# Scores of the dilated groups 4 and 16: query parts stacked on 128 rows, keys doubled, scores emitted further behind their projections

## The chip, the core and the metric

The kernel runs on one core of a Trainium2 chip. A core has a matrix engine (TensorE, PE in the profile; its weight loads are listed apart as PEld), a vector engine (VectorE, DVE), a scalar engine (ScalarE, ACT), a general engine (GpSimd, POOL), a queue that mostly issues DMAs (SyncE, SP), and 16 DMA engines. The engines run beside each other. Each takes its own instructions in the order of the program and waits on semaphores for the others. Matrix products land in 8 banks of PSUM, everything else lies in SBUF, 128 partitions wide. The metric is the device time of one execution in microseconds (us).

## What is computed

The reference is an encoder of two layers over 512 positions of width 1024. Each layer projects its normed input, runs a multi-head latent attention (8 heads, "m" below) and a dilated window attention (three groups of 8 heads, "d" below), gates both, and projects back. The change is in the scores of two of the three dilated groups:

```
DIL_PAIRS = ((128, 1), (512, 4), (2048, 16))      # (window, dilation)

for g, (window, dil) in enumerate(DIL_PAIRS):
    q = partial_rope(qkv[:, :, g, 0], cos, sin)
    k = partial_rope(qkv[:, :, g, 1], cos, sin)
    v = qkv[:, :, g, 2]
    o, lse = banded_attention(to_strided(q, dil), to_strided(k, dil), to_strided(v, dil), window // (2 * dil))
...
s = jnp.einsum('nbqhd,nbkhd->nbhqk', qp, kw) * (Dh ** -0.5)       # Dh = 64
s = jnp.where(valid, s, -inf);  e = exp(s - max(s));  o = (e / sum(e)) v
```

A head is 64 wide, and everything is float32.

## The kernel before

**Precision.** A float32 value is kept as two parts of the faster matrix type: hi, its rounding, and lo, the rest. `split` makes them with one ACT copy (L222) and one DVE subtraction (L223). A product is then hi·hi + hi·lo + lo·hi, which `triple` issues as three matmuls (L242 to L244).

**The units of dilated attention.** `unit(u)` maps 12 units of a layer to a group g and a pair of heads p. Units 0, 1, 6, 7 are the near group (dilation 1); units 2, 3, 8, 9 (dilation 4) and 4, 5, 10, 11 (dilation 16) are the far ones, 8 in each layer. For each unit `dil_qk` projects the query and the key of the two heads (24 matmuls of 512 columns each), rotates them in `rope` (DVE L634, L635, L638, POOL L636), and splits them: the query into a tile `q` (three buffers, shared with the latent attention), the key into the one tile `kst`. In both, head a lies on partitions 64a to 64a+63, and the second index says hi or lo.

**The scores of a far unit.** `far_scores` runs twice for each unit (part 0 and 1). A part has two blocks j of 128 positions. For each block and head there is one matmul of 64 rows and 256 columns (L752: q hi against k hi and k lo) and one of 64 rows and 128 columns (L755: q lo against k hi, added to the first half). That makes 8 matmuls in a part, and 32 parts in the kernel. The two heads of a block have a bank each. DVE adds the mask (L758) and the two halves and takes the row's extreme (L761), ACT takes the exponential (L765).

**What follows.** `far_out` transposes the probabilities on PE (L457), splits them to `pt` and multiplies them with the values (L793). The latent heads do the same with L457 and L558. For dilation 16, `shares` combines the three groups' denominators, and POOL scales the probabilities (L773). `mla_out` gates a pair of latent heads (L441) and splits the result into `hl` tiles, which the output projection reads.

**What sets the order.** `Weave.run` writes the program. It walks a hand-made list of projections (`forward_order`, the main line), and behind each step emits side work that has come due: a side task may start once its needs were emitted at least a lag ago, on a clock that counts estimated PE time. The scores wait `LD` = 8.25 behind the emission of their projections (`LD0` for unit 0, `LM` for latent heads). Where the main line is blocked, side tasks are forced without regard to the lag: the key projection of unit u waits until the scores of unit u-1 are emitted, since there is only one `kst`. Weight tiles are fetched three ahead by SP, split by ACT (L199, L201), and for most of them POOL issues a second, adding DMA that makes the lo part (L202).

Of the kernel before, what the change touches and what calls it, by code (L numbers as in the profile page):

```python
# [8 lines left out]
FR = mybir.dt.float32r  # L9
I32 = mybir.dt.int32  # L10
AF = mybir.ActivationFunctionType
ALU = mybir.AluOpType
AX = mybir.AxisListType

S = 512
# [7 lines left out]
AHEAD, RATE, LAG, CAP = 3, 451.1, 2.5, 34.9  # L23
STEP, LD0, WARM, LG2, LY = 2, 10.0, 8, 16.5, 5.0
LV = 3.0
LG, LP, LD, LM, LC, LN, LX, LF = 6.0, 0.25, 8.25, 2.0, 14.25, 5.75, 5.0, 0.25
SHUF = [i + 8 if i < 8 else i - 8 if i < 16 else i for i in range(32)]

# [4 lines left out]
def unit(u):  # L33

    return u % 6 // 2, 2 * (u // 6) + u % 2
# [26 lines left out]
def F(a):  # L62
    return a.bitcast(F32)
# [74 lines left out]
def hybrid_encoder(ctx, tc, xT, wst, gains, fgain, tables, keytab, masks, out):  # L138
    nc = tc.nc
    PSUM = bass.MemoryType.PSUM  # L140
    const = ctx.enter_context(tc.tile_pool(name="const", bufs=1))
# [6 lines left out]
    def t(shape, dtype, tag, bufs):  # L148
        uid[0] += 1
        return sb.tile(shape, dtype, name=f"{tag}_{uid[0]}", tag=tag, bufs=bufs)  # L150
# [16 lines left out]
    def bank():  # L167
        uid[0] += 1
        return ps.tile([128, S], F32, name=f"bank_{uid[0]}", tag="bank", bufs=8)
# [7 lines left out]
    msk = const.tile([128, 644], F32, name="msk")  # L177
    cms = const.tile([128, 2, S], F32, name="cms")
    kcs = const.tile([128, 8, 32], F32, name="kcs")
    kst = const.tile([128, 2, S], FR, name="kst")  # L180
    kml = [const.tile([128, 2, S], FR, name=f"kml{i}") for i in range(2)]
    x1d = dram.tile([D, S], F32, name="x1d")
    shd = [[dram.tile([24, 128], F32, name=f"shd{l}{p}") for p in range(4)] for l in range(DEPTH)]
# [37 lines left out]
    def split(dst_hi, dst_lo, src):  # L221
        nc.scalar.copy(dst_hi, src)  # L222
        nc.vector.tensor_tensor(dst_lo, src, F(dst_hi), op=ALU.subtract)  # L223
# [119 lines left out]
    def half_chunks(L, key):  # L343

        a = bank()
        for i in range(2):
            w = weight(L.l, *key, i)
            for j in range(0, 4, STEP):
                cost = quads(a, w, L.h[4 * i + j:4 * i + j + STEP], 4 * i + j, 8)
                if i == 0 or j + STEP < 4:  # L350
                    yield cost, 0.0
        return a
# [295 lines left out]
    def dil_qk(L, u, qk):  # L648
        g, p = unit(u)
        a = yield from half_chunks(L, ("dqk", u, qk))  # L650
        if qk == 0:
            f = rope(L, a, "nat" if g else "queries")
            q = t([128, 2, S], FR, "q", 3)
            split(q[:, 0], q[:, 1], f)
            L.q["d", u] = q
        else:
            f = rope(L, a, "nat" if g else "keys")
            split(kst[:, 0], kst[:, 1], f)
        yield 0.65 * STEP, 0.0

    def near_scores(L, u, part):

        g, p = unit(u)
        q = L.q["d", u]
        if part == 0:
            L.st0[p] = t([128, 4, 4], F32, "st0", 2)
        st = L.st0[p]
        banks = [bank() for _ in range(2)]  # L670
        for j in range(2):
            i = 2 * part + j
            for x, (lq, lk) in enumerate(((0, 0), (0, 1), (1, 0))):
                for a in range(2):
                    r = slice(64 * a, 64 * a + 64)
                    so, k = banks[a][:, 256 * j:256 * j + 256], kst[r, lk]
                    if i:
                        k = k[:, 128 * (i - 1):128 * (i + 1)]
                    else:
                        so, k = so.rearrange("p (c x) -> p c x", c=2), k.rearrange("p (c x) -> p c x", c=4)[:, 0:4:3]  # L680
                    nc.tensor.matmul(so, q[r, lq, 128 * i:128 * i + 128], k, start=x == 0, stop=x == 2)  # L681
        for j in range(2):
            i = 2 * part + j
            m = msk[:, 0:256] if i else msk[:, 256:512]
            pt = t([128, S], F32, "p", 8)
            for a in range(2):
                pa = pt[:, 256 * a:256 * a + 256]
                nc.vector.tensor_tensor_reduce(pa, banks[a][:, 256 * j:256 * j + 256], m, -0.125, 3e38,
                                               ALU.add, ALU.min, st[:, i, a:a + 1])
            for a in range(2):  # L690
                pa = pt[:, 256 * a:256 * a + 256]
                nc.scalar.activation(pa, pa, AF.Exp, bias=st[:, i, a:a + 1], scale=-1.0,
                                     accum_out=st[:, i, 2 + a:3 + a])
            L.p["d", u, i] = pt
        if part:
            by_residue(L, p)
        yield 0.9, 1.0
# [37 lines left out]
    def far_scores(L, u, part):  # L735

        g, p = unit(u)
        q = L.q["d", u]  # L740
        st = L.st[p][:, :, g]
        m = msk[:, 512:640].rearrange("p (x y) -> p x y", y=4) if g == 1 else msk[:, 640:644].unsqueeze(1).to_broadcast([128, 32, 4])
        pt = t([128, S], F32, "p", 8)
        p4 = pt.rearrange("p (j a x) -> p j a x", j=2, a=2)
        banks = [bank() for _ in range(2)]
        by4 = lambda x: x.rearrange("p j (x y) -> p j x y", y=4)
        for j in range(2):
            b = 2 * part + j
            c = slice(128 * b, 128 * b + 128)
            for a in range(2):  # L750
                so = banks[a][:, 256 * j:256 * j + 256].rearrange("p (l x) -> p l x", l=2)
                nc.tensor.matmul(so, q[64 * a:64 * a + 64, 0, c], kst[64 * a:64 * a + 64, :, c], start=True, stop=False)  # L752
            for a in range(2):
                so = banks[a][:, 256 * j:256 * j + 128]
                nc.tensor.matmul(so, q[64 * a:64 * a + 64, 1, c], kst[64 * a:64 * a + 64, 0, c], start=False, stop=True)  # L755
        for a in range(2):
            s = banks[a].rearrange("p (j l x) -> p j l x", j=2, l=2)
            nc.vector.tensor_tensor(by4(p4[:, :, a]), by4(s[:, :, 0]), m.unsqueeze(1).to_broadcast([128, 2, 32, 4]), op=ALU.add)  # L758
            for j in range(2):
                b = 2 * part + j  # L760
                nc.vector.tensor_tensor_reduce(p4[:, j, a], s[:, j, 1], p4[:, j, a], -0.125, 3e38, ALU.add, ALU.min,  # L761
                                               st[:, b, a:a + 1])
            for j in range(2):
                b = 2 * part + j
                nc.scalar.activation(p4[:, j, a], p4[:, j, a], AF.Exp, scale=-1.0, bias=st[:, b, a:a + 1],  # L765
                                     accum_out=st[:, b, 2 + a:3 + a])
        L.p["d", u, part] = pt
        if g == 2 and part:
            shares(L, p)
            for b in range(4):  # L770
                for a in range(2):
                    pt = L.p["d", u, b // 2][:, 256 * (b % 2) + 128 * a:256 * (b % 2) + 128 * a + 128]
                    nc.gpsimd.tensor_scalar(pt, pt, L.share[p][:, b, 2, a:a + 1], 0.0, op0=ALU.mult, op1=ALU.add)  # L773
        yield 0.44, 0.5
# [161 lines left out]
    main, nline, sline, tline, cline = ([] for _ in range(5))  # L936
    for L in layers:
        l = L.l
        L.wo, L.x, L.acc, L.o = {}, [], {}, {}
        k = lambda *a: (l,) + a  # L940
        now = lambda *labels: [(x, 0.0) for x in labels]
        later = lambda *labels: [(x, LAG) for x in labels]
        task = lambda line, label, needs, f, *a: line.append((label, needs, lambda f=f, L=L, a=a: f(L, *a)))
# [3 lines left out]
        for o in ORDER:  # L947
            kind, a = o[0], o[1:]
# [8 lines left out]
            elif kind == "nv":  # L957
                task(main, k("nva", *a), now(k("norm")), near_values, a[0])
                task(nline, k(*o), [(k("nva", *a), LV)], turn_values, a[0])
            elif kind == "mv":  # L960
# [12 lines left out]
        for hd in range(8):  # L973
            p = hd // 2
# [3 lines left out]
        for u in range(12):  # L978
            g, p = unit(u)
            i = at["dqk", u, 1]  # L980
            att.append((i, ("d", u), [k("dqk", u, 0), k("dqk", u, 1), k("v", g, p // 2) if g else k("nv", p)],
                        far_scores if g else near_scores, far_out if g else near_out))
        for p in range(4):
            of = {unit(u): u for u in range(12)}
            i = at["dqk", of[2, p], 1]
            needs = later(k("s", "d", of[2, p]), *[k("o", "d", of[g, p]) for g in range(2)])
# [3 lines left out]
        before = [[], []]  # L990
        for _, (what, n), needs, scores, f in sorted(att, key=lambda x: x[0]):
            if scores:
                task(sline, k("s0", what, n), [(x, LM if what == "m" else LD0 if n == 0 else LD) for x in needs], scores, n, 0)
                task(sline, k("s", what, n), now(*before[0]), scores, n, 1)
                task(tline, k("o", what, n), [(k("s", what, n), LG2 if what == "d" and unit(n)[0] == 2 else LG)], f, n)
                before = [before[1], [("t", l, what, n)]]
            else:
                task(cline, k(what, n), needs, f, n)
# [145 lines left out]
```

## Time and profile before

| | |
|---|---|
| time, median of 3 runs | 933.5 us (932.68 to 936.16) |
| the profiled execution's own time | 936.2 us |
| its span, from first to last instruction | 934.4 us |
| mean granted PE clock in it | 0.995 |
| PE matmuls in it | 5172 |
| L752 and L755 among them | 128 and 128 |

A row of the timeline gives the start in us from the span's start, the duration in us, the engine, the line, the operation and its tiles, how many equal ones are merged, and in square brackets how long the engine stood idle before it and what ended that. A row of the groups gives the shapes (for a matmul: contraction rows * output rows, then rows x columns of the moving operand), the count, the busy time of the group in us (overlap counted once), the mean duration of one in ns, and the idle time before them. Matmuls are pipelined: the duration of one is its way through the array, and what a stream of them costs is the distance from start to start.

### The profile page before, as it was taken

The page shows a single profiled execution, that of the slowest core. Times are in us where ns is not written, and L with a number is a line of the kernel's source. Part 1 is how long each engine was busy: PE and PEld are TensorE (multiplying, and loading weights), DVE is VectorE, ACT ScalarE, POOL GpSimd, SP SyncE. Part 2 cuts the span into 40 slices and gives each one's busy share as a digit, 9 for nine tenths or more (in the row PEclk, how much of TensorE's full clock was granted, in tenths as well). Part 3 has the DMA queues.
Part 4 walks back from the last instruction along what each step waited for, and adds up shares of the span by engine and source line. Part 5 has one row for each costly group of instructions (what it writes and reads, how often), then busy time and mean ns, then how long its engine had stood idle before and what let it go on. Part 6 is the DMA issues. An engine that isn't in the chain of part 4 may idle for free.

```text
span 934.4 us, 15835 instructions
## 1 busy us (share of the span) xinstructions
PE 910.4 (97%) x5172; PEld 775.1 (83%) x5172; DVE 690.9 (74%) x1732; ACT 597.8 (64%) x1448; POOL 315.1 (34%) x367
## 2 busy tenths in 40 slices
PE   8999999999999999999999999999999999999996
PEld 6978888988889889887897888888888888897775
DVE  6756787877868766688766578797778776757864
ACT  6546776666857766754454578666767586676533
POOL 0034253344542431333312444423554234224300
PEclk9999999999999999999999999999999999999999
DMA  7357453276554764655553854516666557366432
GB/s 272 115 121 141 105 122 68 66 161 147 122 123 93 149 131 104 136 147 147 171 155 104 163 121 86 114 46 138 139 129 148 131 101 148 84 144 144 130 123 90
DMA packets 85746, 118.66 MB, mean 127 GB/s; under 512 B 16864, under 2 KB 34848, under 8 KB 85664
## 3 DMA queue, kind: packets, MB, share of 16 engines
q1 hardware_dynamic: 65648, 81.80, 29.8%
q0 software_dynamic: 19584, 35.66, 24.2%
q8 instruction: 41, 0.67, 0.3%
q14 instruction: 41, 0.34, 0.1%
q10 hardware_dynamic: 432, 0.20, 0.1%
HBM read 113.26 MB, written 4.36 MB: 126 GB/s over the span
## 4 chain that ended last, share of the span: by engine, by line
PE 81%; DVE 8%; ACT 4%; DMA 3%; issue 3%; POOL 1%; ACTq 0%; DVEq 0%; POOLq 0%
PE bank L242 22%; PE bank L244 22%; PE bank L243 22%; PE bank L457 5%; PE bank L558 3%; PE bank L752 1%; PE bank L793 1%; PE bank L681 1%; DMA whl<-wst 1%; DVE pt L223 1%; DMA wraw<-wst 1%; ACT whl L199 1%; DVE tmp L638 1%; POOL tmp L636 1%; DVE whl L204 1%
## 5 line engine op out<-in xcount | busy, mean ns | idle before, releaser
L242 PE MATMUL bank<-hl,whl 128*128 128x512 f32 x728 | 290.2, 399 | 2.2 <-ACT hl L222 1.4
L244 PE MATMUL bank<-hl,whl 128*128 128x512 f32 x728 | 284.4, 391 | 2.0 <-DMA whl<-wst 2.0
L243 PE MATMUL bank<-hl,whl 128*128 128x512 f32 x728 | 284.5, 391 | 0.0
L199 ACT CAST whl<-wraw 128x512 fp32r<-128x512 f32 (+3 forms) x243 | 143.8, 596 | 119.4 <-PE bank L244 77.5
L202 POOL DMA_DIRECT2D whl<-wst x136 | 119.7, 889 | 223.9 <-ACT whl L201 161.5
L244 PEld LDWEIGHTS bank<-hl,whl 128*128 128x128 f32 x728 | 136.7, 188 | 32.5 <-DMA whl<-wst 2.9
L242 PEld LDWEIGHTS bank<-hl,whl 128*128 128x128 f32 x728 | 136.6, 188 | 29.2 <-ACT hl L222 1.8
L243 PEld LDWEIGHTS bank<-hl,whl 128*128 128x128 f32 x728 | 137.0, 188 | 24.6 <-DVE hl L223 0.3
L242 PE MATMUL bank<-whl,hl 128*128 128x256 f32 (+2 forms) x328 | 99.8, 304 | 1.5 <-ACT hl L222 1.5
L244 PE MATMUL bank<-whl,hl 128*128 128x256 f32 (+2 forms) x328 | 98.3, 300 | 0.0
L243 PE MATMUL bank<-whl,hl 128*128 128x256 f32 (+2 forms) x328 | 98.1, 299 | 0.0
L204 DVE TENSOR_TENSOR whl<-wraw,whl 128x512 fp32r<-128x512 f32 (+3 forms) x107 | 76.1, 717 | 26.0 <-ACT whl L199 25.0
L636 POOL TENSOR_TENSOR tmp<-tmp,sd 128x512 f32<-128x512 f32 x48 | 63.2, 1316 | 89.5 <-DVE tmp L634 65.4
L223 DVE TENSOR_TENSOR pt<-bank,pt 128x512 fp32r<-128x512 f32 x128 | 83.6, 684 | 5.6 <-ACT pt L222 4.2
L201 ACT ACTIVATE whl<-wraw 128x512 fp32r<-128x512 f32 x136 | 86.3, 635 | 0.1
L222 ACT CAST pt<-bank 128x512 fp32r<-128x512 f32 x128 | 69.9, 588 | 10.7 <-PE bank L457 10.3
L538 POOL TENSOR_SCALAR p<-p,lc 128x512 f32<-128x512 f32 x64 | 48.9, 771 | 71.4 <-DVE lc L537 70.6
L457 PE MATMUL bank<-ident,p 128*128 128x128 f32 x512 | 67.7, 275 | 0.0
L242 PEld LDWEIGHTS bank<-whl,hl 128*128 128x128 f32 x328 | 62.5, 191 | 3.9 <-ACT hl L222 1.8
L244 PEld LDWEIGHTS bank<-whl,hl 128*128 128x128 f32 x328 | 62.5, 191 | 2.0 <-DVE hl L223 0.4
L243 PEld LDWEIGHTS bank<-whl,hl 128*128 128x128 f32 x328 | 62.5, 191 | 1.7
L457 PEld LDWEIGHTS bank<-ident,p 128*128 128x128 f32 x512 | 59.2, 142 | 5.4
(178 smaller groups left out, 1612.5 us busy)
## 6 DMA issues: line engine op xcount, KB each, us to landing
wraw<-wst SPq DMA_DIRECT2D x218, 256.0 KB, 2.9
whl<-wst POOLq DMA_DIRECT2D x136, 256.0 KB, 4.5
tmp<-shd SPq DMA_DIRECT2D x32, 128.0 KB, 4.4
xl<-xT SPq DMA_DIRECT2D x10, 256.0 KB, 2.7
wraw<-wst SPq DMA_DIRECT2D x16, 144.0 KB, 2.2
wraw<-wst SPq DMA_DIRECT2D x12, 192.0 KB, 2.6
x1d<-xl SPq DMA_DIRECT2D x8, 256.0 KB, 2.9
xl<-x1d SPq DMA_DIRECT2D x8, 256.0 KB, 3.0
```

What stands on the lines that cost most here:

```text
L199: nc.scalar.copy(hi, src)
L201: nc.scalar.mul(lo, src, -1.0)
L202: nc.gpsimd.dma_start(lo, wst[l * len(PLAN) + i, :, :c], accum_op=ALU.add)
L204: nc.vector.tensor_tensor(lo, src, F(hi), op=ALU.subtract)
L222: nc.scalar.copy(dst_hi, src)
L223: nc.vector.tensor_tensor(dst_lo, src, F(dst_hi), op=ALU.subtract)
L242: nc.tensor.matmul(a, w[:, 0], h[:, 0], start=first, stop=False)
L243: nc.tensor.matmul(a, w[:, 0], h[:, 1], start=False, stop=False)
L244: nc.tensor.matmul(a, w[:, 1], h[:, 0], start=False, stop=last)
L457: nc.tensor.transpose(b[:, 128 * i:128 * i + 128], x, ident)
L538: nc.gpsimd.tensor_scalar(pt, pt, l1, 0.0, op0=ALU.mult, op1=ALU.add)
L636: nc.gpsimd.tensor_tensor(u, u, L.sd, op=ALU.mult)
```

## The change

The far queries are stored differently. Column plane i of the tile now belongs to head i: the head's hi part lies on its own 64 partitions, its lo part on the other 64. That takes two ACT copies and two DVE subtractions on 64 partitions where there was one of each on 128. The keys get a tile twice as large, with a plane for each head: the head's hi and lo on its own partitions, split in halves like the query, and a copy of both on the other 64 partitions, which two POOL instructions make (64 partitions x 1024 elements). A block and head then need one matmul of 128 rows and 256 columns, which multiplies hi and lo of the query with k hi and k lo at once (lo·lo comes with it). The bank now holds both heads of one block instead of one head of both blocks. The scores of far units become due 10.75 instead of 8.25 behind their projections. The near units keep their form.

```diff
+LDF = 10.75
...
-    kst = const.tile([128, 2, S], FR, name="kst")
+    kst = const.tile([128, 2, 2, S], FR, name="kst")
...
             q = t([128, 2, S], FR, "q", 3)
-            split(q[:, 0], q[:, 1], f)
+            if g == 0:
+                split(q[:, 0], q[:, 1], f)
+            else:
+                for i in range(2):
+                    hi, lo = slice(64 * i, 64 * i + 64), slice(64 - 64 * i, 128 - 64 * i)
+                    nc.scalar.copy(q[hi, i], f[hi])
+                    nc.vector.tensor_tensor(q[lo, i], f[hi], F(q[hi, i]), op=ALU.subtract)
...
-            split(kst[:, 0], kst[:, 1], f)
+            if g == 0:
+                split(kst[:, 0, 0], kst[:, 1, 0], f)
+            else:
+                for i in range(2):
+                    r = slice(64 * i, 64 * i + 64)
+                    split(kst[r, 0, i], kst[r, 1, i], f[r])
+                    nc.gpsimd.tensor_scalar(kst[64 - 64 * i:128 - 64 * i, :, i], F(kst[r, :, i]), 1.0, 0.0,
+                                            op0=ALU.mult, op1=ALU.add)
...
-        banks = [bank() for _ in range(2)]
-        by4 = lambda x: x.rearrange("p j (x y) -> p j x y", y=4)
         for j in range(2):
             b = 2 * part + j
-            c = slice(128 * b, 128 * b + 128)
+            s, c = bank().rearrange("p (a l x) -> p a l x", a=2, l=2), slice(128 * b, 128 * b + 128)
             for a in range(2):
-                so = banks[a][:, 256 * j:256 * j + 256].rearrange("p (l x) -> p l x", l=2)
-                nc.tensor.matmul(so, q[64 * a:64 * a + 64, 0, c], kst[64 * a:64 * a + 64, :, c], start=True, stop=False)
+                nc.tensor.matmul(s[:, a], q[:, a, c], kst[:, :, a, c], start=True, stop=True)
...
             for a in range(2):
-                so = banks[a][:, 256 * j:256 * j + 128]
-                nc.tensor.matmul(so, q[64 * a:64 * a + 64, 1, c], kst[64 * a:64 * a + 64, 0, c], start=False, stop=True)
...
-                task(sline, k("s0", what, n), [(x, LM if what == "m" else LD0 if n == 0 else LD) for x in needs], scores, n, 0)
+                task(sline, k("s0", what, n), [(x, LM if what == "m" else LD0 if n == 0 else LD if unit(n)[0] == 0 else LDF) for x in needs], scores, n, 0)
```

The masks, the row extremes and the exponentials keep their number and shapes, regrouped by block. Line numbers of the changed kernel are one higher from L26 to the middle of `dil_qk` (L242 to L244 become L243 to L245, L457 and L558 become L458 and L559) and five higher behind `far_scores` (L793, L797 and L799 become L798, L802 and L804).

**Three places of the order.** The first is on PE, in layer 0, at the first part of unit 10 (head pair 2, dilation 16). Before, between rows of a projection:

```order
L244 MATMUL bank_4555<-hl_156,whl_4460 128x512
L752 MATMUL bank_4569<-kst,q_3884 128x256
L752 MATMUL bank_4570<-kst,q_3884 128x256
L755 MATMUL bank_4569<-kst,q_3884 128x128
L755 MATMUL bank_4570<-kst,q_3884 128x128
L752 MATMUL bank_4569<-kst,q_3884 128x256
L752 MATMUL bank_4570<-kst,q_3884 128x256
L755 MATMUL bank_4569<-kst,q_3884 128x128
L755 MATMUL bank_4570<-kst,q_3884 128x128
L242 MATMUL bank_4555<-hl_165,whl_4460 128x512
```

And now, at the same part:

```order
L244 MATMUL bank_4549<-hl_180,whl_4481 128x512
L245 MATMUL bank_4549<-hl_180,whl_4481 128x512
L763 MATMUL bank_4581<-kst,q_3878 128x256 x2
L763 MATMUL bank_4589<-kst,q_3878 128x256 x2
L798 MATMUL bank_4598<-pt_4515,v_3583 128x256 x2
L243 MATMUL bank_4549<-hl_183,whl_4481 128x512
```

Eight rows became four, and the part moved 12 projection matmuls further behind its key, to a place ahead of a value product (L798).

The second place is on PE too, in layer 0, at the first part of unit 2, the first far unit. Its query is projected after its key, shortly ahead. Before, the score rows stand between transposes of one latent half-head and the value products (L558) of that half-head:

```order
L457 MATMUL bank_1554<-ident,p_1286 128x128
L752 MATMUL bank_1563<-kst,q_1507 128x256
L752 MATMUL bank_1564<-kst,q_1507 128x256
L755 MATMUL bank_1563<-kst,q_1507 128x128
L755 MATMUL bank_1564<-kst,q_1507 128x128
L752 MATMUL bank_1563<-kst,q_1507 128x256
L752 MATMUL bank_1564<-kst,q_1507 128x256
L755 MATMUL bank_1563<-kst,q_1507 128x128
L755 MATMUL bank_1564<-kst,q_1507 128x128
L558 MATMUL bank_1545<-pt_1551,v_1157 128x256 x4
L558 MATMUL bank_1545<-pt_1559,v_1157 128x256 x4
L457 MATMUL bank_1591<-ident,p_1308 128x128
```

Now:

```order
L458 MATMUL bank_1560<-ident,p_1286 128x128
L763 MATMUL bank_1569<-kst,q_1511 128x256
L763 MATMUL bank_1577<-kst,q_1511 128x256
L763 MATMUL bank_1569<-kst,q_1511 128x256
L763 MATMUL bank_1577<-kst,q_1511 128x256
L559 MATMUL bank_1551<-pt_1557,v_1157 128x256
L458 MATMUL bank_1593<-ident,p_1308 128x128
L458 MATMUL bank_1593<-ident,p_1317 128x128
L458 MATMUL bank_1593<-ident,p_1308 128x128
L458 MATMUL bank_1593<-ident,p_1317 128x128
```

The scores stand where they stood (here the main line was blocked, and the longer lag does not count), but seven of the eight value products now stand behind the next eight transposes.

The third place is on DVE, at the end of layer 0, from the last far scores (unit 11, part 1) to the gating of the last latent heads. Before, directly behind that part's L761 rows:

```order
L223 TENSOR_TENSOR pt_4928<-bank_4923,pt_4928 128x512
L809 TENSOR_REDUCE mm_4904<-st_3966 128x8
L223 TENSOR_TENSOR pt_4936<-bank_4931,pt_4936 128x512
L811 TENSOR_TENSOR e_4906<-mm_4904,st_3966 128x24
L839 TENSOR_TENSOR og_3809<-og_3809,tmp_4813 128x512
L814 TENSOR_TENSOR el_4909<-e_4906,st_3966 128x24
L839 TENSOR_TENSOR og_4635<-og_4635,tmp_4814 128x512
L816 TENSOR_REDUCE ls_4911<-el_4909 128x8
L431 TENSOR_TENSOR tmp_4948<-bank_4819,rb_448 128x512
L817 RECIPROCAL ls_4911<-ls_4911 128x8
L441 SCALAR_TENSOR_TENSOR tmp_4953<-mo_3357,gate_4552 128x512
```

Now, from behind the first part's L767 rows:

```order
L224 TENSOR_TENSOR pt_4887<-bank_4882,pt_4887 128x512
L224 TENSOR_TENSOR pt_4895<-bank_4890,pt_4895 128x512
L844 TENSOR_TENSOR og_3803<-og_3803,tmp_4817 128x512
L844 TENSOR_TENSOR og_4597<-og_4597,tmp_4818 128x512
L765 TENSOR_TENSOR p_4901<-bank_4902,msk 128x256
L765 TENSOR_TENSOR p_4901<-bank_4910,msk 128x256
```

The four large operations moved ahead of the second part's masks (L765); behind those masks stand four L767, one L802, one L814, and then the gating, now L442.

More of the change, by code (lines that the diff above doesn't have):

```diff
@@ L675, in near_scores @@
                     r = slice(64 * a, 64 * a + 64)
-                    so, k = banks[a][:, 256 * j:256 * j + 256], kst[r, lk]
+                    so, k = banks[a][:, 256 * j:256 * j + 256], kst[r, lk, 0]
                     if i:
@@ L744, in far_scores @@
         p4 = pt.rearrange("p (j a x) -> p j a x", j=2, a=2)
-        banks = [bank() for _ in range(2)]
-        by4 = lambda x: x.rearrange("p j (x y) -> p j x y", y=4)
         for j in range(2):
             b = 2 * part + j
-            c = slice(128 * b, 128 * b + 128)
+            s, c = bank().rearrange("p (a l x) -> p a l x", a=2, l=2), slice(128 * b, 128 * b + 128)
             for a in range(2):
-                so = banks[a][:, 256 * j:256 * j + 256].rearrange("p (l x) -> p l x", l=2)
-                nc.tensor.matmul(so, q[64 * a:64 * a + 64, 0, c], kst[64 * a:64 * a + 64, :, c], start=True, stop=False)
+                nc.tensor.matmul(s[:, a], q[:, a, c], kst[:, :, a, c], start=True, stop=True)
+            by4 = lambda x: x.rearrange("p a (x y) -> p a x y", y=4)
+            nc.vector.tensor_tensor(by4(p4[:, j]), by4(s[:, :, 0]), m.unsqueeze(1).to_broadcast([128, 2, 32, 4]), op=ALU.add)
             for a in range(2):
-                so = banks[a][:, 256 * j:256 * j + 128]
[L755 to L761, printed above, removed]
+                nc.vector.tensor_tensor_reduce(p4[:, j, a], s[:, a, 1], p4[:, j, a], -0.125, 3e38, ALU.add, ALU.min,
                                                st[:, b, a:a + 1])
-            for j in range(2):
-                b = 2 * part + j
+            for a in range(2):
                 nc.scalar.activation(p4[:, j, a], p4[:, j, a], AF.Exp, scale=-1.0, bias=st[:, b, a:a + 1],
```

## Prediction

> **What bounds the kernel now.** The page first, for the shares of the engines and the chain that ended last.
>
> ```profile
> span 934.4 us, 15835 instructions
> ...
> PE 910.4 (97%) x5172; PEld 775.1 (83%) x5172; DVE 690.9 (74%) x1732; ACT 597.8 (64%) x1448; POOL 315.1 (34%) x367
> ...
> PE 81%; DVE 8%; ACT 4%; DMA 3%; issue 3%; POOL 1%; ACTq 0%; DVEq 0%; POOLq 0%
> ```
>
> PE is busy nearly all the time and makes up 81% of the chain. Next I asked what PE waits for (the view of the waits, PE alone; its two longest rows: total, times, longest).
>
> ```profile
> PE bank L242 <- ACT hl L222: 2.9, 2, 1.5
> ...
> PE bank L244 <- DMA whl<-wst: 2.0, 2, 1.4
> ```
>
> No wait is worth more than 3 us in the whole kernel. So time falls where PE's own work falls, and rises where a change makes PE wait. DVE, ACT and POOL have room on average; what counts for them is when single results are wanted.
>
> **The score matmuls.** What a part of the scores costs is not its busy time but what it pushes apart. The timeline of PE around the first part of unit 10 in layer 0, amid projection matmuls:
>
> ```profile
> 387.47 0.39 PE L244 MATMUL bank<-hl,whl 128*128 128x512 f32 x1
> 387.78 0.39 PE L752 MATMUL bank<-kst,q 64*128 64x256 f32 x2
> 388.01 0.22 PE L755 MATMUL bank<-kst,q 64*128 64x128 f32 x2
> 388.07 0.33 PE L752 MATMUL bank<-kst,q 64*128 64x256 f32 x2
> 388.23 0.22 PE L755 MATMUL bank<-kst,q 64*128 64x128 f32 x2
> 388.39 0.50 PE L242 MATMUL bank<-hl,whl 128*128 128x512 f32 x1
> 388.72 0.40 PE L243 MATMUL bank<-hl,whl 128*128 128x512 f32 x1
> ```
>
> And around a value product, which has the form that the scores get: 128 rows, 256 columns, new weights for each matmul, columns read in two pieces of 128.
>
> ```profile
> 419.15 0.39 PE L244 MATMUL bank<-hl,whl 128*128 128x512 f32 x1
> 419.38 0.40 PE L793 MATMUL bank<-pt,v 128*128 128x256 f32 x2
> 419.61 0.39 PE L242 MATMUL bank<-hl,whl 128*128 128x512 f32 x1
> 419.85 0.40 PE L243 MATMUL bank<-hl,whl 128*128 128x512 f32 x1
> ```
>
> In the second window a 512-column matmul takes 0.23 from start to start, and the two of L793 take 419.61 - 419.38 = 0.23, so 0.118 each, with nothing lost ahead or behind. In the first, L244 takes 387.78 - 387.47 = 0.31 and L242 takes 388.72 - 388.39 = 0.33: 0.08 lost on the way into the 64-row form and 0.10 on the way out. From L244 to L243 it is 1.25; less two 512-column matmuls (0.46) the part costs 0.79. Four matmuls of the new form cost 4 x 0.118 = 0.47. That saves 0.32 a part, and PE has nothing else to do in that time. **Term A: 32 parts x 0.32 = 10.2 us faster.** Its bounds are 0.13 (only the body from 387.78 to 388.39, 0.61, shrinks and the losses at both ends stay) and 0.32; I take 0.32, since the row of L793 shows no such losses behind the same neighbour.
>
> The Trainium skill, page "TensorEngine Tiling (Array Packing)", section "Key Properties", says that changing the tiling mode drains the TensorE. The trace agrees, with the 0.08 and 0.10 above. By a rule that counted the drain out, the part would save only 0.61 - 0.47 = 0.14, and term A would be 4.5.
>
> **The extra splits.** The groups by shape, for the present splits and for splits of 64 partitions:
>
> ```profile
> L223 DVE TENSOR_TENSOR q<-tmp,q 128x512 fp32r<-128x512 f32 x24 | 18.4, 765 | 3.3 <-ACT q L222 2.7
> ...
> L223 DVE TENSOR_TENSOR kst<-tmp,kst 128x512 fp32r<-128x512 f32 x24 | 16.5, 687 | 7.0 <-ACT kst L222 6.6
> ...
> L222 ACT CAST kst<-tmp 128x512 fp32r<-128x512 f32 x24 | 14.9, 621 | 39.4 <-DVE tmp L638 26.0 <-DVE tmp L642 13.4
> L222 ACT CAST q<-tmp 128x512 fp32r<-128x512 f32 x24 | 14.9, 621 | 30.2 <-DVE tmp L638 15.8 <-DVE tmp L645 13.1 <-PE bank L244 1.2
> ...
> L223 DVE TENSOR_TENSOR q<-mn,q 64x512 fp32r<-64x512 f32 x16 | 11.2, 697 | 3.5 <-ACT q L222 3.3
> ...
> L222 ACT CAST q<-mn 64x512 fp32r<-64x512 f32 x16 | 9.9, 616 | 0.9 <-DVE mn L499 0.7
> ```
>
> Half the partitions cost the same time, so each of the 16 queries and 16 keys costs one more operation on either engine: 32 x 0.70 = 22 us on DVE (691 becomes 713, 76%) and 32 x 0.62 = 20 us on ACT (66%). On the path they matter only as latency: the second half of a query is ready about 0.7 later. For the copies on POOL, these groups:
>
> ```profile
> L202 POOL DMA_DIRECT2D whl<-wst x136 | 119.7, 889 | 223.9 <-ACT whl L201 161.5 <-ACT v L615 18.4 <-DVE pt L223 18.2
> ...
> L636 POOL TENSOR_TENSOR tmp<-tmp,sd 128x512 f32<-128x512 f32 x48 | 63.2, 1316 | 89.5 <-DVE tmp L634 65.4 <-PE bank L457 8.7 <-DVE smy L404 5.9
> ...
> L538 POOL TENSOR_SCALAR p<-p,lc 128x512 f32<-128x512 f32 x64 | 48.9, 771 | 71.4 <-DVE lc L537 70.6
> ...
> L520 POOL TENSOR_SCALAR q<-mr 32x1024 fp32r<-32x1024 f32 x16 | 18.0, 1125 | 9.0 <-DVE mr L223 7.7 <-PE bank L755 0.3
> ```
>
> No row has 64 partitions; nearest is L520, the same operation on 1024 elements between partitions, 1.125. Bounds: 0.77 (L538, 512 elements) and 1.32 (L636, two inputs). So 32 x 1.125 = 36 us, on an engine that is idle for two thirds. Queued behind a copy, which waits for DVE's split, stand the adding weight DMAs (L202) and the next rotation (L636). The DMAs have 161.5 us of idle time ahead of them in which POOL waits for ACT anyway, and are issued three tiles ahead; I cost them at nothing. If that cover is gone, the wait of 2.0 for such tiles (L244, above) may double: -2.0.
>
> **Where a result is now wanted sooner than it comes.** First the keys. By the order, the scores of units 9, 10 and 11 moved about 1.5 to 3 us further behind the key, which pays for the 2.3 that the two copies add. Those of unit 8 did not move, since the main line is blocked there. Its rows:
>
> ```profile
> 344.98 0.62 ACT L222 CAST kst<-tmp 128x512 fp32r<-128x512 f32 x1 [1.64 <-DVE tmp L638]
> ...
> 345.72 0.69 DVE L223 TENSOR_TENSOR kst<-tmp,kst 128x512 fp32r<-128x512 f32 x1
> ...
> 348.04 0.38 PE L752 MATMUL bank<-kst,q 64*128 64x256 f32 x2
> ...
> 349.15 1.28 POOL L636 TENSOR_TENSOR tmp<-tmp,sd 128x512 f32<-128x512 f32 x1 [4.15 <-DVE tmp L634]
> ```
>
> POOL is free then. DVE's first half ends at 346.41, the copies at 347.54 and 348.66, and the second matmul (head 1) would start at 348.16: it waits 0.5. **Term C: 2 layers x 0.5 = 1.0 slower**, between 0 (copies of 0.77 end at 347.95) and 1.8 (copies of 1.32 end at 349.05).
>
> Second the query of unit 2, which PE waits for already:
>
> ```profile
> 132.75 0.92 DVE L223 TENSOR_TENSOR q<-tmp,q 128x512 fp32r<-128x512 f32 x1
> 132.78 0.38 PE L752 MATMUL bank<-kst,q 64*128 64x256 f32 x2
> 133.72 0.33 PE L755 MATMUL bank<-kst,q 64*128 64x128 f32 x2 [0.55 <-DVE q L223]
> ...
> 135.04 1.22 PE L558 MATMUL bank<-pt,v 128*128 128x256 f32 x7 [0.45 <-DVE pt L223]
> ...
> 138.89 0.79 PE L242 MATMUL bank<-kml,q 96*128 96x512 f32 x1
> ```
>
> These scores did not move either (blocked again). From 132.78 to 138.89 it is 6.1 us, for two parts, 8 value products and 8 transposes that take about 3.2 undisturbed. Now the first matmul can start at about 133.6, when the first half's subtraction is done, and the second head's at 134.35; the transposes, which stand ahead of seven value products now, fill the wait for `pt`, which comes 0.7 later. I put the end at 4.4 after 132.78: 1.7 less than before, of which A holds 0.6. **Term B: 1.0 faster**, in layer 0 alone; bounds -1.4 (a subtraction of 0.7 more that nothing fills, in both layers) and +2.7.
>
> Third the ends of the layers, where the output projection waits for the gated latent heads (`hl`):
>
> ```profile
> 412.36 0.39 PE L752 MATMUL bank<-kst,q 64*128 64x256 f32 x2
> ...
> 414.21 0.74 DVE L758 TENSOR_TENSOR p<-bank,msk 128x256 f32<-128x256 f32 x2
> ...
> 420.33 1.21 DVE L441 SCALAR_TENSOR_TENSOR tmp<-mo,gate 128x512 f32<-128x512 f32 x1
> ...
> 422.77 0.73 PE L242 MATMUL bank<-hl,whl 128*128 128x512 f32 x2 [1.38 <-ACT hl L222]
> ...
> 878.94 0.50 PE L242 MATMUL bank<-whl,hl 128*128 128x512 f32 x1 [1.54 <-ACT hl L222]
> ```
>
> From the last far scores (412.36) to `hl` it is 10.4 us, and PE stood 1.4 there and 1.5 in layer 1. By the order now, with each PE row at its distance, `hl` is wanted 6.6 after those scores instead of 8.9. Five large DVE operations of 0.69 no longer stand between them: 10.4 - 3.5 = 6.9. But four of them now stand ahead of the second part's masks, so that these begin about 2.9 after their scores instead of 1.85 (414.21): 8.0, a wait of 1.4 as before. If the gate and four value sums queued ahead have DVE 2.4 behind, it is 3.8. I take 2.5. **Term D: 2 x 1.1 = 2.2 slower**, between 2.9 faster (no wait is left) and 4.6 slower.
>
> **The sum.** 10.2 + 1.0 - 1.0 - 2.2 = 8.0 us. The profiled execution took 936.2 (span 934.4 and 1.8 around it) and becomes 928.2. The median of the runs is 2.7 below that execution; from 933.5 the forecast is **925.5 us**.
>
> **The rivals.** First, *the late results eat it*: B, C and D at their bad ends and the weight tiles late leave 10.2 - 1.4 - 1.8 - 4.6 - 2.0 = 0.4, so 933.1; with half of that loss, 929. For it: the far units cost DVE and ACT 1.3 more each just where DVE is already the one that PE waits for, and at units 2 and 8 the longer lag does not do what it says. Against it: all these waits together are some 7 us now.
>
> Second, *the kernel gets slower because the tiled form was the better one*. A pair of 64-row matmuls starts together (x2 in a row above). If the 0.79 of a part is not the form's but comes with the operands (`kst` and `q`, fresh weights), then the pairs' columns cost 2 x 0.118 + 2 x 0.059 = 0.35, the operands 0.44, and the new part 0.47 + 0.44 = 0.91: 32 x 0.12 = 3.8 slower, with C and D 940.5. It decides from 0.2 us for a new matmul on. Against it: L793 and L558 have fresh weights too and show no such loss. The Trainium skill, page "TensorE: Matmul & The Clock Gate", section "Why this matters for your kernels", advises this way: matmuls of few rows on distinct row groups, so that they run at once. The trace agrees that they do, but shows the price of the form beside it.
>
> **How the numbers follow.** The forecast has 0.76; 925.5 with its terms a little off, 921 to 930. The first rival has 0.18, the second 0.06. Best ends of A to D give 917.7, worst 933.1; leaving out a tenth on either side, the range is **920.5 to 932.0**. A measurement of this kernel tells about 0.5% (4.7 us) from no change. Faster than 928.8: the forecast but for its upper edge, **0.70**; within 0.5%: **0.24**; slower: the second rival, **0.06**.
>
> **What would show it.** In the changed profile: 128 score matmuls of form 128*128 128x256 with 0.118 from start to start and neighbours of 0.23 (A); POOL copies of about 1.1, and PE waiting some 0.5 for them at unit 8 only (C); fewer idle stretches between unit 2's scores and the next latent scores (B); waits for `hl` of 2 to 3 us at both layer ends (D). The prediction is wrong if a score matmul takes 0.2 or more, if PE waits for copies at other units, or if DVE's extra splits make PE wait for `pt` or for banks along the layers.

## The result

The changed kernel takes **962.9 us** (median of 4 runs, 959.4 to 967.1) against 934.8 us for the kernel before (4 runs): a ratio of 1.0305, 95% interval 1.026 to 1.0349. It is 28 us slower, where 925.5 (920.5 to 932.0) was forecast. The profiled execution took 959.4 us with a span of 957.6, against 934.4 before: 23.2 us longer.

### The profile page after: what moved, and what is told of

Its sections match the earlier page's. It is cut to its first block, busy times and chain, and to the rows that moved or that the text cites. A ratio compares the mean times of both kernels' runs of the same rounds, so it can differ in the third digit from the quotient of the medians.

```text
span 957.6 us, 15689 instructions
## 1 busy us (share of the span) xinstructions
PE 911.9 (95%) x5044; PEld 780.9 (82%) x5044; DVE 720.4 (75%) x1764; ACT 620.2 (65%) x1480; POOL 351.4 (37%) x399
## 4 chain that ended last, share of the span: by engine, by line
PE 71%; DVE 12%; ACT 6%; issue 4%; POOL 4%; DMA 2%; ACTq 0%; POOLq 0%; DVEq 0%
PE bank L243 20%; PE bank L245 20%; PE bank L244 20%; PE bank L458 4%; PE bank L559 3%; POOL tmp L637 1%; DMA wraw<-wst 1%; PE bank L763 1%; DVE tmp L802 1%; DVE pt L224 1%; DVE og L804 1%; DVE q L661 1%; PE bank L798 1%; ACT p L537 1%; PE bank L695 1%
## 5 line engine op out<-in xcount | busy, mean ns | idle before, releaser
L243 PE MATMUL bank<-hl,whl 128*128 128x512 f32 x728 | 290.2, 399 | 0.9 <-DVE st L702 0.6
L245 PE MATMUL bank<-hl,whl 128*128 128x512 f32 x728 | 285.3, 392 | 3.6 <-DMA whl<-wst 3.6
L244 PE MATMUL bank<-hl,whl 128*128 128x512 f32 x728 | 285.3, 392 | 0.0
L245 PEld LDWEIGHTS bank<-hl,whl 128*128 128x128 f32 x728 | 137.4, 189 | 33.8 <-DMA whl<-wst 4.0
L243 PEld LDWEIGHTS bank<-hl,whl 128*128 128x128 f32 x728 | 137.6, 189 | 27.7 <-PE bank L245 1.5
L244 PEld LDWEIGHTS bank<-hl,whl 128*128 128x128 f32 x728 | 137.7, 189 | 24.4
L243 PE MATMUL bank<-whl,hl 128*128 128x256 f32 (+2 forms) x328 | 99.3, 304 | 0.0
L244 PE MATMUL bank<-whl,hl 128*128 128x256 f32 (+2 forms) x328 | 98.4, 300 | 0.0
L245 PE MATMUL bank<-whl,hl 128*128 128x256 f32 (+2 forms) x328 | 98.2, 299 | 0.0
L205 DVE TENSOR_TENSOR whl<-wraw,whl 128x512 fp32r<-128x512 f32 (+3 forms) x107 | 78.2, 737 | 23.7 <-ACT whl L200 22.6
L202 ACT ACTIVATE whl<-wraw 128x512 fp32r<-128x512 f32 x136 | 86.3, 634 | 0.3
L458 PE MATMUL bank<-ident,p 128*128 128x128 f32 x512 | 68.7, 277 | 0.0
L458 PEld LDWEIGHTS bank<-ident,p 128*128 128x128 f32 x512 | 60.2, 143 | 5.3
L244 PEld LDWEIGHTS bank<-whl,hl 128*128 128x128 f32 x328 | 62.7, 191 | 2.2 <-DVE whl L205 0.3
L243 PEld LDWEIGHTS bank<-whl,hl 128*128 128x128 f32 x328 | 62.7, 191 | 1.8
L245 PEld LDWEIGHTS bank<-whl,hl 128*128 128x128 f32 x328 | 62.7, 191 | 1.7
```

The lines of the kernel that those rows point to most:

```text
L202: nc.scalar.mul(lo, src, -1.0)
L205: nc.vector.tensor_tensor(lo, src, F(hi), op=ALU.subtract)
L243: nc.tensor.matmul(a, w[:, 0], h[:, 0], start=first, stop=False)
L244: nc.tensor.matmul(a, w[:, 0], h[:, 1], start=False, stop=False)
L245: nc.tensor.matmul(a, w[:, 1], h[:, 0], start=False, stop=last)
L458: nc.tensor.transpose(b[:, 128 * i:128 * i + 128], x, ident)
```

## The profile after

The page, and the granted clock:

```profile
span 957.6 us, 15689 instructions
...
PE 911.9 (95%) x5044; PEld 780.9 (82%) x5044; DVE 720.4 (75%) x1764; ACT 620.2 (65%) x1480; POOL 351.4 (37%) x399
...
PE 71%; DVE 12%; ACT 6%; issue 4%; POOL 4%; DMA 2%; ACTq 0%; POOLq 0%; DVEq 0%
```

```profile
core 0: 957.6 us, clock 0.984
```

PE is idle for 957.6 - 911.9 = 45.7 us instead of 24.0, and the granted clock fell from 0.995 to 0.984. PE has 128 matmuls less, yet is busy 1.5 us longer. The chain now runs through DVE, ACT and POOL for 22% (13% before). What PE waits for (total, times, longest):

```profile
PE bank L798 <- DVE pt L224: 6.8, 2, 3.4
PE bank L763 <- DVE q L661: 6.5, 6, 2.1
PE bank L763 <- POOL kst L671: 4.8, 6, 0.9
PE bank L245 <- DMA whl<-wst: 3.6, 1, 3.6
PE bank L559 <- DVE pt L224: 2.7, 4, 0.7
```

Three of the five are far scores, or what far scores feed; L559 is the value product of a latent half-head, and L245 waits for a weight tile. Where nothing is late, the scores are as cheap as forecast. Unit 10 in layer 0, PE's timeline:

```profile
394.81 0.39 PE L245 MATMUL bank<-hl,whl 128*128 128x512 f32 x1
395.04 0.63 PE L763 MATMUL bank<-kst,q 128*128 128x256 f32 x4
395.51 0.40 PE L798 MATMUL bank<-pt,v 128*128 128x256 f32 x2
395.74 0.40 PE L243 MATMUL bank<-hl,whl 128*128 128x512 f32 x1
```

Four matmuls take 395.51 - 395.04 = 0.47, with nothing lost ahead or behind (0.23 from L245 to L763). So the form keeps its promise, and something else costs some 33 us.

**An account.** For every matmul I took the distance to the next start, less the undisturbed distance for its form (0.228 for 512 columns, 0.118 for 256, 0.113 for a transpose), and added what is over 0.3 us as *waits*. *Clock* is half of the time at which 0.5 of the clock was granted. What is left between the first and the last start is PE's *own work*; 8.9 us lie outside (up to 9.9 in the runs below). It is good to about 2 us.

| profiled span, us | span | waits | clock | own work |
|---|---|---|---|---|
| before | 934.4 | 20.2 | 3.4 | 901.9 |
| changed | 957.6 | 43.3 | 13.7 | 891.8 |
| difference | +23.2 | +23.1 | +10.3 | -10.1 |

By place, both layers together, waits and clock rose by about 11 us at the layer ends, 6 at units 2 and 3, 6 at unit 8, 6 at one late weight tile, 3 at units 4 and 5, and 1.5 at the start.

## Experiments

Three theories stood against each other: L, the longer lag; K, the latency of the new operands; X, the throughput of the extra operations. Each run is compared with runs of the kernel before on the same chip (medians 935.0, 934.7 and 935.3 in the three groups).

### The change taken apart

*lag_alone* is the kernel before with the lag only, *form_old_lag* the changed kernel without it:

```diff
+LDF = 10.75            # lag_alone: in the kernel before, for far units
-LDF = 10.75            # form_old_lag: in the changed kernel
+LDF = 8.25
```

*extra_unread* is the kernel before with the change's extra operations, into a tile that nobody reads (for far units; the query has the split alone):

```diff
+                split(dum[0:64, 0], dum[0:64, 1], f[0:64])
+                for i in range(2):
+                    nc.gpsimd.tensor_scalar(dum[64:128], F(kst[64 * i:64 * i + 64]), 1.0, 0.0, op0=ALU.mult, op1=ALU.add)
```

*hi_copies* shortens the copies and starts them earlier, at the old lag:

```diff
-                    split(kst[r, 0, i], kst[r, 1, i], f[r])
-                    nc.gpsimd.tensor_scalar(kst[64 - 64 * i:128 - 64 * i, :, i], F(kst[r, :, i]), 1.0, 0.0,
+                    nc.scalar.copy(kst[r, 0, i], f[r])
+                    nc.gpsimd.tensor_scalar(kst[64 - 64 * i:128 - 64 * i, 0, i], F(kst[r, 0, i]), 1.0, 0.0,
                                             op0=ALU.mult, op1=ALU.add)
+                    nc.vector.tensor_tensor(kst[r, 1, i], f[r], F(kst[r, 0, i]), op=ALU.subtract)
```

> The kernel before with nothing changed but the lag of the far scores, 10.75 instead of 8.25. Theory L (the longer lag makes the end of each layer and the blocked places run out of cover, PE waits there and its clock is halved after the long waits): slower by 8 to 20 us, 942 to 955, with waits of 2 us or more for pt or hl at both layer ends. Theory K (the new operands, halved splits and POOL copies, come too late) and theory X (the extra operations fill DVE, ACT and POOL): no change, 932 to 938.

> The changed kernel with the lag of the far scores back at 8.25. Theory L: the waits at the layer ends fall back to those of before and the cheaper score matmuls show, 922 to 930. Theory K: PE waits for the POOL copies at units 8 to 11 and for the query at unit 2, as in the changed kernel or longer, 950 to 970. Theory X: 945 to 965, with the waits spread over many lines.

> The kernel before, score form and lag untouched, which makes 32 more 64-row splits (ACT and DVE) and 32 POOL copies of 64 x 1024 elements into a tile that nobody reads. Theory X: slower by 10 us or more, 945 to 960. Theories L and K: 933 to 938, the operations lie beside PE's work.

> The changed kernel at the old lag 8.25, with copies of the keys' hi part alone (64 x 512 elements), started right behind ACT's hi part instead of behind DVE's subtraction; the lo half that the copy would fill holds zeros, so lo times lo is left out. The second key half is ready about 1.7 us sooner. Theory K: 922 to 932 and at least 10 us below the run with full copies and the old lag. Theory L: within 4 us of that run. Theory X: 940 to 960.

| run | median, us | ratio to before (95%) | waits | clock | own work |
|---|---|---|---|---|---|
| lag_alone | 953.2 | 1.0196 (1.0152 to 1.0240) | 30.9 | 10.2 | 899.4 |
| form_old_lag | 944.2 | 1.0107 (1.0079 to 1.0135) | 33.1 | 8.5 | 892.3 |
| extra_unread | 954.0 | 1.0197 (1.0168 to 1.0225) | 30.2 | 10.2 | 901.8 |
| hi_copies | 940.1 | 1.0058 (1.0039 to 1.0078) | 31.5 | 5.1 | 892.4 |

No theory is right alone. The lag costs 18 us with the old form, the extra operations 19 us with the old form and the old lag. With the cheaper form, 10.1 by the account, that makes +18 +19 -10 = +27, against the +28 measured. The runs with the new form fit the same sum: form_old_lag is 9 slower than before (19 - 10), and the changed kernel 962.9 - 944.2 = 18.7 slower than form_old_lag (the lag). Own work falls by about 10 in both runs that have the new form, and by less than 3 in the other two. lag_alone came out as L had it (about 2.9 of waits at either layer end, though in layer 1 the trace puts it down to a DMA) and extra_unread as X had it. form_old_lag met no theory: X's 945 to 965 was nearest, L's 922 to 930 far off. The copies' latency is the smallest part: shorter and earlier copies bring 4 us, where K asked for 10, and as they are shorter they also leave POOL less work. PE's waits in form_old_lag say the same:

```profile
PE bank L763 <- DVE q L661: 6.5, 6, 2.1
...
PE bank L763 <- POOL kst L671: 3.1, 4, 0.8
```

The query, late from DVE, is the larger wait, not the copied keys.

### Where the extra operations cost

*extra_2_3* makes the unread operations at units 2 and 3 alone; *extra_splits* and *extra_copies* make one kind of them, at all far units. *form_not_2_3* is form_old_lag with units 2 and 3 in the form of before (splits, keys and scores).

```diff
-            if g:
+            if u in (2, 3):                    # extra_2_3, at both places
-            if g == 0:
+            if g == 0 or u in OLD:             # form_not_2_3, OLD = (2, 3), and likewise in far_scores
```

> The kernel before with the unread splits and POOL copies of the run extra_unread, but at units 2 and 3 alone: 8 of the 32 extra splits and 8 of the 32 copies. Theory H (hot spot: what the extra operations cost falls at units 2 and 3, where PE already waits for the query and the next latent half-heads, with the halved clock behind it): at least 13 of the 19 us stay, 947 to 954. Theory X (they cost a little everywhere): a quarter of the 19, 938 to 941.

> The kernel before with the 32 unread 64-row splits (ACT copy and DVE subtraction) of the run extra_unread and no POOL copies. If DVE's and ACT's extra operations carry the cost: 948 to 954. If the copies on POOL carry it (they stand ahead of the rotation of the next query and of the lo parts of weight tiles): 934 to 938.

> The kernel before with the 32 unread POOL copies of the run extra_unread and no extra splits. If DVE's and ACT's extra operations carry the cost: 933 to 937. If POOL's copies carry it: 945 to 953.

> The changed kernel at the old lag 8.25, with units 2 and 3 in the form of before (splits, keys and score matmuls). Theory H: 944 falls by the hot spot's 13 to 17 us less 2.6 for the 8 parts that lose the cheaper form, 928 to 934. Theory X: the splits and copies left out are a quarter, 944 to 946 falls by 5 less 2.6, 940 to 943.

| run | median, us | ratio to before (95%) | waits | clock | own work |
|---|---|---|---|---|---|
| extra_2_3 | 946.2 | 1.0119 (1.0085 to 1.0153) | 26.6 | 5.1 | 902.3 |
| extra_splits | 946.8 | 1.0133 (1.0104 to 1.0162) | 26.4 | 6.8 | 902.1 |
| extra_copies | 940.1 | 1.0051 (1.0034 to 1.0068) | 24.2 | 3.4 | 901.9 |
| form_not_2_3 | 936.8 | 1.0016 (0.9998 to 1.0034) | 26.0 | 5.1 | 893.5 |

A quarter of the operations brings 12 of the 19 us: less than the 13 that theory H asked for, far more than the quarter of X. Taking units 2 and 3 out of the new form brings 7 us back, between what the two theories had. The splits cost 12 and the copies 5; my two expectations had put it all on one. So most of it is one hot spot. PE there in extra_unread, where the operations are not even waited for:

```profile
134.42 0.38 PE L759 MATMUL bank<-kst,q 64*128 64x256 f32 x2 [1.09 <-ACT q L223]
...
138.31 1.01 PE L559 MATMUL bank<-pt,v 128*128 128x256 f32 x3 [1.78 <-DVE pt L224]
```

The wait for `pt` was 0.45 before. On DVE, the unread subtraction stands ahead of it:

```profile
135.42 1.52 DVE L224 TENSOR_TENSOR dum<-tmp,dum 64x512 fp32r<-64x512 f32 x1
...
137.58 1.28 DVE L224 TENSOR_TENSOR pt<-bank,pt 128x512 fp32r<-128x512 f32 x2
```

It takes 1.52 here (why it isn't 0.69 is in the last section), and the wait grew by 1.33, most of its length. The wait of 1.09 for the query itself comes from further ahead; term B below follows the same chain.

### Where the lag costs

Both runs are the kernel before with the longer lag at some far units only (the diff is against lag_alone):

```diff
-LD if unit(n)[0] == 0 else LDF
+LDF if n in (2, 3, 8, 9, 10) else LD         # lag_not_4_5_11
+LDF if n in (2, 3, 8, 9) else LD             # lag_2_3_8_9
```

> The kernel before with the lag of 10.75 for far units 2, 3, 8, 9 and 10 alone; units 4, 5 and 11 keep 8.25. Theory E (the longer lag costs at two places in each layer: the latent scores queued behind units 4 and 5, and the layer end behind unit 11): 934 to 938. Rival (the longer lag costs at every unit, or moves the weight tiles' order): 5 of 8 of the 18 us stay, 944 to 948.

> The kernel before with the lag of 10.75 for far units 2, 3, 8 and 9 alone. Theory E2 (the longer lag costs where later scores queue behind it with an end that doesn't move: unit 10 held unit 11 back at the layer end, units 4 and 5 the latent scores behind them): 933 to 938. Rival (it costs at every unit): half of the 18 us stay, 942 to 945.

lag_not_4_5_11 took 947.9 us (1.0139, 1.0103 to 1.0175), which theory E did not allow. It lies in the range of its rival, 944 to 948; but lag_2_3_8_9 took 935.4 (0.9995, 0.998 to 1.001), as E2 had it, and that excludes a cost at every unit. The profile of the first showed why E had picked the wrong units:

```profile
PE bank L794 <- DVE pt L224: 11.3, 2, 5.6
```

That is still the layer end, and longer: `Weave` takes score tasks from one list in order, so unit 10's lag held unit 11 back. With unit 10 at the old lag too, nothing is left of the 18 us. The longer lag is free at units 2, 3, 8 and 9. Where it costs, in lag_alone, PE at the end of layer 0:

```profile
418.94 0.23 PE L756 MATMUL bank<-kst,q 64*128 64x128 f32 x2
422.04 0.80 PE L794 MATMUL bank<-pt,v 128*128 128x256 f32 x2 [2.86 <-DVE pt L224]
```

The last scores of the layer and the next value products stand back to back. Before, 24 projection matmuls and 8 transposes stood between them. The other place is the transposes of a latent half-head, whose scores are queued behind those of units 4 and 5; this wait is gone in both runs that spare these units:

```profile
PE bank L458 <- ACT p L537: 4.7, 2, 2.7
```

### What is left when the costs are taken out

*hi_not_2_3* is hi_copies with units 2 and 3 in the form of before; *hi_not_2_3_lag7* is the same with a shorter lag for the far scores.

```diff
+            if g == 0 or u in OLD:             # OLD = (2, 3)
-LDF = 8.25
+LDF = 7.25                                    # hi_not_2_3_lag7
```

> The run hi_copies (old lag, hi parts alone copied, lo times lo left out) with units 2 and 3 in the form of before. Theory H: 24 parts save 0.32 each, 7.7 us, and the waits are those of before: 926 to 930, faster than both kernels. Theory X: 936 to 940.

> The run hi_not_2_3 with the lag of the far scores at 7.25 instead of 8.25. If the waits that are left lie at the layer ends, scores emitted sooner shorten them: 928 to 932. If the copies' latency is what is left, PE waits for them at more units: 935 to 942.

933.5 us (0.9983, 0.9965 to 1.0001) and 934.3 (0.9988, 0.9972 to 1.0004): neither can be told from the kernel before, and both lie between the ranges that their theories had. In hi_not_2_3 own work is 896.0, a gain of 5.9 of the 7.7 that 24 parts should bring, and waits are 24.4 against 20.2. So even then about two thirds of the gain shows up again as small waits. A version that beats the kernel before was not found.

## Why the prediction was wrong, step by step

Two steps failed above all. The lag was taken as free, and alone it costs 18 us. The extra operations were taken to matter "only as latency" on the path, with their other effects at nothing; unread, where nothing waits for their results, they cost 19 us.

**Term A (10.2 faster) was right.** A part costs 0.47, and own work fell by 10.1. That excludes the second rival (0.12 a part slower, own work up by 3.8). The Trainium skill, page "TensorEngine Tiling (Array Packing)", section "Key Properties", has the drain at a change of the tiling mode. The rows here agree with it: the 0.08 and 0.10 at the two ends go with the form, and are more than half of the 0.32 gained.

**Term D (2.2 slower) failed most.** I followed the distance from the last scores to `hl` and forecast waits for `hl`. The wait comes earlier, and for `pt`:

```profile
417.90 0.62 PE L763 MATMUL bank<-kst,q 128*128 128x256 f32 x3 [0.85 <-POOL kst L671]
...
420.50 0.47 PE L763 MATMUL bank<-kst,q 128*128 128x256 f32 x2 [1.01 <-DVE og L804]
421.21 0.50 PE L763 MATMUL bank<-kst,q 128*128 128x256 f32 x2 [0.23 <-DVE tmp L432]
425.13 0.80 PE L798 MATMUL bank<-pt,v 128*128 128x256 f32 x2 [3.42 <-DVE pt L224]
```

Before, the value product stood 7.0 us behind these scores (412.36 to 419.38); now it is the next row. The order on record showed the other side of it, four large DVE operations moved ahead of the masks; I read that as a loss of 1.1, since I had not looked at what stood on PE between these two rows. With the waits for a copy and for banks, waits and clock rose by 11 us over both layers. "Pays for the 2.3 that the two copies add" is where the lag was taken as free. It did not even pay for the copies at unit 11, whose scores are these: PE waited 0.85 for one.

**Term B (1.0 faster) had the wrong sign.** Waits at units 2 and 3 rose by 6. POOL, DVE and PE at unit 2:

```profile
133.31 2.49 POOL L521 TENSOR_SCALAR q<-mr 32x1024 fp32r<-32x1024 f32 x2
```

```profile
132.42 0.69 DVE L639 TENSOR_TENSOR tmp<-tmp,tmp 128x512 f32<-128x512 f32 x1 [1.54 <-POOL tmp L637]
...
133.94 2.39 DVE L661 TENSOR_TENSOR q<-tmp,q 64x512 fp32r<-64x512 f32 x2
```

```profile
135.03 0.47 PE L763 MATMUL bank<-kst,q 128*128 128x256 f32 x2 [2.07 <-DVE q L661]
...
136.48 0.47 PE L763 MATMUL bank<-kst,q 128*128 128x256 f32 x2 [0.97 <-DVE q L661]
```

And DVE before:

```profile
131.22 0.69 DVE L638 TENSOR_TENSOR tmp<-tmp,tmp 128x512 f32<-128x512 f32 x1 [0.86 <-POOL tmp L636]
```

I had the scores at about 133.6 and 134.35, where PE came to them at 132.78: 0.8 and 1.6 late. Now PE comes to them at 135.03 - 2.2 = 132.8 (2.2 by the account), and they start at 135.03 and 136.48: 2.2 and 3.7 late. Two steps failed. A subtraction takes 2.39 / 2 = 1.2 here, not 0.69. And the last operation of the rotation (L639), from which I counted, came at 132.42 instead of 131.22. That began with the key, 9 us earlier. Now, all engines:

```profile
123.54 1.85 DVE L224 TENSOR_TENSOR kst<-tmp,kst 64x512 fp32r<-64x512 f32 x2
...
126.74 0.69 ACT L537 ACTIVATE p<-bank,nm 128x512 f32<-128x512 f32 x1 [0.78 <-DVE nm L534]
...
130.15 0.90 POOL L203 DMA_DIRECT2D whl<-wst  x1 [0.29 <-ACT whl L202]
```

Before:

```profile
123.45 0.66 DVE L223 TENSOR_TENSOR kst<-tmp,kst 128x512 fp32r<-128x512 f32 x1
...
125.34 0.69 ACT L536 ACTIVATE p<-bank,nm 128x512 f32<-128x512 f32 x1
...
128.75 0.90 POOL L202 DMA_DIRECT2D whl<-wst  x1 [0.70 <-ACT whl L201]
```

DVE's second key subtraction puts off a latent half-head's row extremes (`nm`) behind it, ACT waits for them and comes 1.4 later to its exponentials and, behind these, to a weight tile's lo part; POOL's adding DMA for that tile comes 1.4 later too, and the query's rotation stands behind it on POOL. POOL's own key copies (124.94 to 127.43) stand in the same queue, and as POOL waited only 0.29 for that tile, they alone would have put the DMA off nearly as far. Either is enough: the last operation of the rotation came at 132.41 in extra_splits and at 132.59 in extra_copies (0.4 and 0.5 of which those runs were late already at 119 us). The step "the DMAs ... I cost them at nothing" asked whether those DMAs would be late themselves, not what stands behind them on POOL.

**Term C (1.0 slower) had the right place and a quarter of the size** of the waits: 2.0 us at unit 8 in each layer by the account, and 1.7 of clock in layer 0 besides. All engines, the rows on the way to the keys, now:

```profile
337.15 1.40 DVE L661 TENSOR_TENSOR q<-tmp,q 64x512 fp32r<-64x512 f32 x2
...
341.62 0.51 ACT L706 ACTIVATE p<-p,st 128x256 f32<-128x256 f32 x1 [0.49 <-DVE st L702]
...
344.12 0.63 ACT L202 ACTIVATE whl<-wraw 128x512 fp32r<-128x512 f32 x1
...
345.05 0.86 POOL L203 DMA_DIRECT2D whl<-wst  x1 [8.51 <-ACT whl L202]
...
347.26 0.69 DVE L639 TENSOR_TENSOR tmp<-tmp,tmp 128x512 f32<-128x512 f32 x1 [2.89 <-POOL tmp L637]
...
349.65 2.58 POOL L671 TENSOR_SCALAR kst<-kst 64x1024 fp32r<-64x1024 f32 x2 [1.59 <-DVE kst L224]
...
351.15 0.39 PE L763 MATMUL bank<-kst,q 128*128 128x256 f32 x1 [0.83 <-POOL kst L671]
...
352.28 0.62 PE L763 MATMUL bank<-kst,q 128*128 128x256 f32 x3 [0.74 <-POOL kst L671]
```

And before:

```profile
334.93 0.69 DVE L223 TENSOR_TENSOR q<-tmp,q 128x512 fp32r<-128x512 f32 x1
...
338.57 0.51 ACT L692 ACTIVATE p<-p,st 128x256 f32<-128x256 f32 x1 [0.49 <-DVE st L688]
...
341.07 0.63 ACT L201 ACTIVATE whl<-wraw 128x512 fp32r<-128x512 f32 x1
...
344.20 0.69 DVE L638 TENSOR_TENSOR tmp<-tmp,tmp 128x512 f32<-128x512 f32 x1 [2.03 <-POOL tmp L636]
```

A copy took 1.29, not 1.125, and the first score starts 0.2 behind its copy's end. The larger part lies far ahead: the query's second subtraction on DVE (1.40 for both instead of 0.69) puts off the row extremes of a near unit (L702) behind it, ACT waits for them as it did before (0.49 in both), and the tile's lo part (L202) follows 7.0 behind the query's first subtraction instead of 6.1. POOL's adding DMA waits for it, the key's rotation stands behind that DMA, and the key comes 0.9 nearer to its scores: PE came to them at 351.15 - 1.0 = 350.2, 2.9 behind L639, where before it was 348.04 - 344.20 = 3.8 behind L638.

**The first rival** ("late results eat it") was the right mechanism, but its bad ends summed to 9.8 us, where 33 came. (They were not even the worst ends of the working: with A at its own lower bound, 0.13 a part, the 933.1 would have been about 939.) A third of the 33 is the halved clock, which no term held. The late weight tile (3.6 for L245) need not be laid to the change: such waits sum to 4.0 in lag_2_3_8_9, which takes the time of before.

## What to carry to other kernels

When a lag or a form moves work, list for each engine that is waited for what now stands between producer and consumer, at the ends of loops and at blocked places first: back-to-back rows there are the price, however free the engines are on average. An extra operation off the critical path costs its whole length where a queue already has no slack, and it must be followed across queues: here a second subtraction on DVE held up row extremes, these ACT's exponentials and a weight tile, the tile a DMA on POOL, and that the rotation behind it. A saving on the bounding engine spread over 32 places is worth its sum only if no place has its cover taken away.

## What the runs showed of the hardware

**Waits cost twice.** The granted clock fell to 0.5 in whole steps of 3.41 us (up to three in a row, in extra_unread), 1.71 us of work lost in each step. Windows of the changed kernel (length, PE, PEld, DVE, ACT and POOL busy, then the clock, the DMA share and GB/s):

```profile
349.70:353.10 3.40, 1.82 (x11) 1.20 (x10) 3.37 (x6) 1.84 (x4) 2.44 (x2) 1.00 0.81 167
353.10:356.50 3.40, 3.40 (x18) 3.40 (x17) 2.84 (x10) 0.98 (x2) 1.28 (x1) 0.50 0.26 77
421.30:424.70 3.40, 0.41 (x2) 0.20 (x2) 3.27 (x15) 0.83 (x5) 0.00 (x0) 1.00 0.64 180
424.80:428.20 3.40, 3.07 (x8) 2.58 (x9) 3.40 (x13) 1.51 (x8) 1.18 (x1) 0.50 0.00 0
```

And of the kernel before:

```profile
132.77:136.19 3.42, 2.42 (x18) 1.87 (x18) 3.39 (x6) 3.03 (x6) 2.04 (x3) 1.00 0.49 95
136.19:139.60 3.41, 3.41 (x19) 2.87 (x18) 2.78 (x13) 2.50 (x11) 0.57 (x1) 0.50 0.76 126
```

A window in which PE was busy for 0.41 of 3.40 us is followed by one at half clock. So is one with 1.82 of 3.40 busy (349.70), where the two idle stretches were 0.83 and 0.74, and in the kernel before one with 2.42 busy, around the idle stretches of 0.55 and 0.45 at unit 2; one of the changed kernel with 1.76 busy (131.20 to 134.60) is not. The Trainium skill, page "TensorE: Matmul & The Clock Gate", has a free-running window of 3413 ns (section on Part 1, the HAM clock gate), and the trace agrees with that length. In the section "HAM oscillation — how this bites in real kernels" the Trainium skill warns of idle gaps over about 3.4 us; here two gaps of under 1 us in a window were enough in both kernels. What decides is open; PE's busy time alone does not.

**DVE behind a POOL operation.** The group of L661 (shortest, median and longest in ns, first and last start):

```profile
L661 DVE TENSOR_TENSOR q<-tmp,q x32: 685/687/1420, 133.9 to 873.3; 64x512 fp32r<-64x512 f32 x32
```

It took 0.69 in most of its 32 executions, but 1.18 on average in the four beside POOL's copies L521 (1.2 each in the row at 133.94). Beside POOL's key copies L671, the 20 subtractions of `pt` kept their 0.69. That is not a matter of what POOL does: beside the copies at unit 8 (349.65 to 352.23), DVE has both kinds.

```profile
350.22 1.29 DVE L224 TENSOR_TENSOR pt<-bank,pt 128x512 fp32r<-128x512 f32 x2
351.43 1.33 DVE L205 TENSOR_TENSOR whl<-wraw,whl 128x512 fp32r<-128x512 f32 x1
```

The subtractions of `pt` read one input from a PSUM bank and kept their pace; L205 and L661 read both from SBUF. L205 ended 0.53 behind the end of POOL's copy, and in the trace of the changed kernel that is the rule. I took DVE operations on two tensors of 512 columns that began while a POOL operation had 0.2 us or more still to run. All 28 with both inputs in SBUF ended 0.53 to 0.55 behind POOL's end and took 0.74 to 1.79 (left out are those beside L778, whose short operations overlap each other in the record); of the 120 with one input in PSUM that met a POOL operation at all, none took more than 0.70. In the kernel before, 2 of 18 were not held up. So a POOL copy costs DVE time if an operation on two SBUF inputs comes behind its start, and this is part of what the extra operations cost at unit 2, where L661 and the unread subtraction both end 0.5 behind POOL's L521. How large a part was not measured alone.
